# A second level of Strassen-Winograd for two of the seven products in a gate projection

## The chip, the cores and the metric

The kernel runs on one core of a Trainium2 chip. The metric is the device time of one execution in microseconds (us). The engines are TensorE (PE, matrix products), VectorE (DVE), ScalarE (ACT), GpSimd (POOL) and SyncE (SP); DVE, ACT and POOL each work through their instructions in the order of the program, and semaphores make one engine wait for another. DMAs are issued from the queues of SP, ACT and POOL.

## What is computed

With a depth of 1 the reference is one layer, the pooling mixer, between two RMS norms. It has 4096 tokens and a width of 1024, all in float32:

```python
def pool_mixer(h, in_w, group_w, group_b, scale, out_w):
    b, s, _ = h.shape
    u, gate = jnp.split(h @ in_w, 2, axis=-1)
    ug = u.reshape(b, s, POOL_GROUPS, POOL_GROUP_DIM)
    pooled = jnp.stack([trailing_mean(ug[:, :, g], w) for g, w in enumerate(POOL_WINDOWS)],
                       axis=2) - ug
    mixed = jnp.einsum('bsgc,gcd->bsgd', pooled, group_w) + group_b
    y = mixed.reshape(b, s, POOL_WIDTH) * scale * jax.nn.silu(gate)
    return y @ out_w
...
normed = rms_norm(h, norm_w[i])
h = h + pool_mixer(normed, ...)
...
return rms_norm(h, final_norm_w)
```

## The kernel before

**Precision.** Every float32 operand is split in two parts, hi (rounded by an ACT copy, L152) and lo (what is left, a DVE subtraction, L146). A product of operands is three matmuls: hi by hi, hi by lo, lo by hi (`mm3`, L576 to L583). "Splitting" below means such a pair, an ACT copy and a DVE subtraction behind it.

**The seven products.** Each large matrix product is done block by block in the scheme of Strassen and Winograd: the operands are quartered, and seven products P1 to P7 of sums and differences of quarters take the place of eight. P1 is A11 B11 and P7 is S3 T3, where S3 is a difference of quarters of the activations and T3 one of the weights. The activations of one half are two tiles of 128 by 1024.

**Three phases.** First input phase ("a"): the branch that is pooled, 4 blocks of 1024 tokens, with the group map folded into the weights. Second input phase ("b"): the gate, 4 blocks, whose parts of x, normalised in phase a, are read again from memory (`sd`). Output phase ("o"): 8 blocks of 512 tokens. A list of steps (L960 to L962) has 28 products of a, 28 of b and 56 of o; the main loop (L1204) goes through it. In each turn it loads the operands of a step some places ahead, forms sums, splits the operands of the next step, runs the product (`run`, `product_in` at L587) and clears the banks (`evict_in`, L710).

**A product of the input phases** is 48 matmuls of 128 by 512 into four of the eight PSUM banks (`bank_of`, L585: P1, P2, P7 and P4 in banks 0 to 3, the others in banks 4 to 7). Products that follow each other accumulate: P1's result is copied from banks 0 to 3 into 4 to 7 by ACT (L152), P2, P6, P7 and P3 are copied out to SBUF by ACT, P5 and P4 are added to such copies by DVE (L143). In phase b's order, P1, P2, P6, P7, P5, P4, P3, the next block's P1 follows P3.

**Buffers.** The split operands lie in four tiles `op0` to `op3` that are taken in turn (`next_op`, L463), each with hi and lo of one half. All other working tiles come from two sets, 11 `st` tiles and 8 slightly longer `vt` tiles (L112 to L115); a request gets the tile that has been free longest, from the set whose head is older (`take`, L129). A tile's new writer waits for its last reader, a DMA included.

**Statistics.** For blocks 1 to 3 of phase a, the sums of squares come from ACT, the inverse root is finished by POOL (L194 to L212), written to memory (`store_rs`, L421) and read back spread over the partitions (`load_rstd`, L453); both are on POOL's queue. The parts of x are multiplied with it on DVE (`normalize`, L456, its operation at L149) before they are split.

**Weights of phase b** are loaded, formed and split during block 3 of phase a and block 0 of phase b (`load_wb`, `form_wb`, `split_wb`, L262 to L318); T3 is formed and stored earlier (`save_t3`, L274). The output weights are loaded and split in block 3 of phase b (`load_w`, L328).

**The pool stage** (`pool`): the trailing sums as DVE scans (L662), two DVE operations each behind them (L684 and the multiplication at L149), for two groups at once, held back by one or two steps after the product that completes its input (`pool_later`, `pool_due`).

The order of instructions on each engine is made by a scheduler from the program's order; `tc.issue_after` holds an instruction behind another.

Of the kernel before, what the change touches and what calls it, by code (L numbers as in the profile page):

```python
# [10 lines left out]
F32 = mybir.dt.float32  # L11
# [50 lines left out]
def kernel(  # L62
# [48 lines left out]
    ops = [mem.tile([P, 4 * H], F32R, tag=f"op{i}", name=f"op{i}") for i in range(4)]  # L111
# [42 lines left out]
    def split(dst, src):  # L154

        latest_split[1] = copy(dst[:, 0], src).ins
        latest_split[0] = sub(dst[:, 1], src, dst[:, 0].bitcast(F32)).ins
# [10 lines left out]
    wvd = [dram.tile([P, 2, H], F32, name=f"wvd{k}") for k in range(4)]  # L168
    t3d = [dram.tile([P, 2, H], F32, name=f"t3d{h}") for h in range(2)]
# [15 lines left out]
    nc.vector.memset(eps, EPS)  # L185
    scrap = const.tile([P, 1], F32, name="scrap")
# [75 lines left out]
    def load_wb(i):  # L262
        for h in range(2):
            p = parts[i, h] = {}
            if i in (P1, P6):
# [3 lines left out]
            for name, place, used in (("t3", t3d[h], (P6, P7)), ("22", wvd[2 + h], (P5, P3))):  # L269
# [4 lines left out]
    def save_t3():  # L274

        for h in range(2):
# [7 lines left out]
            for u in us:  # L284
                give(u)
# [22 lines left out]
    def split_wb(i):  # L308
        for h in range(2):
            (u,) = parts.pop((i, h)).values()  # L310
            if i == P1:
                split_scaled(w[i][h], u, pair(norm_c, h, 0))
            elif i == P2:
# [147 lines left out]
    turn = [0]  # L461

    def next_op(pattern, **sizes):  # L463
        t = ops[turn[0] % 4]
        turn[0] += 1
        return t.rearrange(pattern, **sizes)
# [3 lines left out]
    def split_halves(us, saved=None, by_pool=False):  # L470
        ts = []
        for h, u in enumerate(us):
            t = next_op("p (s a b) -> p s a b", s=2, a=2)
# [66 lines left out]
    def split_in(q, b, i):  # L540
        s = xs[b]
        key = {P1: "11", P2: "12", P6: "2", P7: "21", P5: "11", P4: "22", P3: "12"}[i]
        later = q == 0 and b == 0 and i in (P1, P2)
# [42 lines left out]

    def product_in(i, t, sets, by_bank, between=None, behind=None):  # L587
        ps = sets[bank_of[i]]
# [3 lines left out]
        for n, (h, ct) in enumerate(halves):  # L592
            if between and n in between:
                between[n]()
            c = slice(ct * P, (ct + 1) * P)
            with tc.issue_after(behind) if behind and n == 1 else nullcontext():
                for kk in range(2):
                    mm3(
                        ps[ct],
                        (w[i][h][:, 0, kk, c], w[i][h][:, 1, kk, c]),  # L600
                        (t[h][:, 0, kk], t[h][:, 1, kk]),
                        i in (P1, P7) and h == 0 and kk == 0,
                        h == 1 and kk == 1,
                    )
        if between and 8 in between:
            between[8]()

# [714 lines left out]
```

## Time and profile before

| | |
|---|---|
| Runs of the kernel before | median 916.3 us, 915.63 to 917.7 (3 runs) |
| The profiled execution | 917.32 us, its span 915.6 us |
| Granted TensorE clock | 0.998 |
| Matmuls 128x512 of the input phases (`bank<-op,w`) | 2688 |
| Read from and written to memory | 115.45 MB and 60.83 MB |
| Second input phase in the trace | about 329 to 620 us |

A row of a group has the line, the engine, the operation, what is written and read (buffer numbers left out), the tile shapes and the count; then its busy time in us, the mean ns of one, and the idle time of its engine just before, with what ended it. Matmuls are pipelined, so the mean of one is longer than their spacing. A row of a timeline has the start and the duration in us. A row of DMA issues has the queue, the count, the KB of one and the median us from the issue to the landing. A row of windows has the window and, for each engine, busy us and instructions.

### The profile page before, as it was taken

What the parts mean: (1) busy time and instruction counts of PE and PEld (TensorE: products, weight loads), DVE (VectorE), ACT (ScalarE), POOL (GpSimd) and SP (SyncE); (2) the same over time, 40 slices, a digit from 0 to 9 for tenths busy, and PEclk for the clock granted to TensorE, in tenths of its full rate; (3) what the DMA queues carried; (4) which work ended last, traced back from release to release, by engine and by line L of the source; (5) the groups of instructions that cost most, each with busy time, mean ns of one, the idle gap of its engine ahead of it and who ended that gap; (6) DMA issues with size and microseconds to landing.
All of it is one profiled execution on the core that took longest, in us unless ns stands there. A gap on an engine that the chain in (4) does not pass through costs nothing.

```text
span 915.6 us, 11210 instructions
## 1 busy us (share of the span) xinstructions
PE 904.4 (99%) x4212; PEld 789.0 (86%) x4212; DVE 703.5 (77%) x769; ACT 457.5 (50%) x741; POOL 52.6 (6%) x130
## 2 busy tenths in 40 slices
PE   9999999999999999999999999999999999999996
PEld 7788888888888888888888888888888888888886
DVE  3898994894699997586696589589978677676675
ACT  7869447447345565246345546654423424324333
POOL 0023201001100000000000000000101101001010
PEclk9999999999999999999999999999999999999999
DMA  9986865666756635016614725745746536356122
GB/s 340 401 320 195 316 236 166 214 230 197 264 198 241 250 146 200 24 47 238 244 47 160 257 87 194 246 161 184 252 165 227 163 135 230 128 194 216 37 92 93
DMA packets 66518, 177.02 MB, mean 193 GB/s; under 512 B 6048, under 2 KB 23840, under 8 KB 66464
## 3 DMA queue, kind: packets, MB, share of 16 engines
q1 hardware_dynamic: 59888, 154.78, 47.9%
q10 hardware_dynamic: 4176, 13.65, 3.8%
q0 software_dynamic: 2400, 7.88, 2.5%
q8 instruction: 33, 0.54, 0.2%
q14 instruction: 21, 0.17, 0.1%
HBM read 115.45 MB, written 60.83 MB: 193 GB/s over the span
## 4 chain that ended last, share of the span: by engine, by line
PE 88%; DMA 5%; DVE 3%; ACT 2%; issue 1%; SPq 0%; DVEq 0%; ACTq 0%
PE bank L581 88%; DMA early<-in_wut 2%; DMA st<-in_x 1%; DMA st<-wvd 1%; DMA st<-in_xt 1%; DVE op L146 1%; DMA t3d<-st 1%; PE bank L374 0%; DVE st L146 0%; DVE st L149 0%; ACT early L408 0%; ACT op L152 0%; DVE st L143 0%; DVE vt L143 0%; DVE vt L146 0%
## 5 line engine op out<-in xcount | busy, mean ns | idle before, releaser
L581 PE MATMUL bank<-op,w 128*128 128x512 f32 x2688 | 581.8, 379 | 2.3 <-DVE op L146 1.5
L581 PEld LDWEIGHTS bank<-op,w 128*128 128x128 f32 x2688 | 507.6, 189 | 75.7 <-DVE op L146 2.3
L581 PE MATMUL bank<-w,op 128*128 128x512 f32 (+1 forms) x1356 | 290.3, 377 | 0.0
L581 PEld LDWEIGHTS bank<-w,op 128*128 128x128 f32 x1356 | 254.6, 189 | 35.8
L146 DVE TENSOR_TENSOR op<-st,op 128x1024 fp32r<-128x1024 f32 x127 | 154.6, 1221 | 75.6 <-ACT op L152 75.5
L152 ACT ACTIVATE op<-st 128x1024 fp32r<-128x1024 f32 x127 | 133.1, 1052 | 143.8 <-PE bank L581 128.5
L152 ACT ACTIVATE vt<-bank 128x512 f32<-128x512 f32 x100 | 56.8, 593 | 49.3 <-PE bank L581 42.4
L152 ACT ACTIVATE op<-vt 128x1024 fp32r<-128x1024 f32 x39 | 40.9, 1055 | 78.8 <-PE bank L581 65.7
L924 DVE TENSOR_TENSOR st<-bank,st 128x512 f32<-128x512 f32 x60 | 41.1, 687 | 29.8 <-PE bank L581 29.4
L146 DVE TENSOR_TENSOR st<-st,st 128x1024 f32<-128x1024 f32 x35 | 42.5, 1221 | 19.3 <-DMA st<-sd 8.6
L146 DVE TENSOR_TENSOR op<-vt,op 128x1024 fp32r<-128x1024 f32 x39 | 47.5, 1222 | 9.5 <-ACT op L152 9.5
L194 POOL TENSOR_SCALAR oms<-oss 128x2 f32<-128x2 f32 x14 | 9.2, 658 | 600.0 <-ACT st L813 593.9
L152 ACT ACTIVATE bank<-bank 128x512 f32<-128x512 f32 x48 | 27.8, 580 | 30.7 <-PE bank L581 27.1
L146 DVE TENSOR_TENSOR w<-st,w 128x1024 fp32r<-128x1024 f32 x21 | 25.5, 1221 | 12.4 <-ACT w L152 12.3
L662 DVE TENSOR_TENSOR_SCAN vt<-vt,bf 128x512 f32<-128x512 f32 x28 | 34.5, 1269 | 0.2 <-ACT vt L152 0.2
L143 DVE TENSOR_TENSOR vt<-bank,vt 128x512 f32<-128x512 f32 (+1 forms) x51 | 33.2, 678 | 1.6 <-PE bank L581 1.6
L924 DVE TENSOR_TENSOR vt<-bank,vt 128x512 f32<-128x512 f32 (+1 forms) x37 | 24.8, 673 | 12.0 <-PE bank L581 11.7
L152 ACT ACTIVATE w<-st 128x1024 fp32r<-128x1024 f32 x21 | 21.9, 1053 | 17.9 <-PE bank L581 14.9
L149 DVE TENSOR_TENSOR st<-st,vt 128x1024 f32<-128x1024 f32 x23 | 27.2, 1219 | 3.1 <-DMA st<-in_xt 3.1
L684 DVE SCALAR_TENSOR_TENSOR vt<-vt,vt 128x1024 f32<-128x1024 f32 x24 | 29.1, 1214 | 0.0
L152 ACT ACTIVATE st<-bank 128x512 f32<-128x512 f32 x30 | 17.5, 595 | 22.7 <-PE bank L581 10.8
L817 DVE SCALAR_TENSOR_TENSOR st<-st,ors,st 128x1024 f32<-128x1024 f32 x17 | 21.4, 1281 | 6.1 <-POOL ors L212 6.1
(130 smaller groups left out, 556.0 us busy)
## 6 DMA issues: line engine op xcount, KB each, us to landing
st<-in_x SPq DMA_DIRECT2D x36, 512.0 KB, 5.0
st<-in_xt SPq DMA_DIRECT2D x29, 512.0 KB, 6.6
st<-sd SPq DMA_DIRECT2D x29, 512.0 KB, 5.0
sd<-st ACTq DMA_DIRECT2D x23, 512.0 KB, 3.7
vt<-in_x SPq DMA_DIRECT2D x21, 512.0 KB, 5.1
st<-yd SPq DMA_DIRECT2D x19, 512.0 KB, 4.3
yd<-vt SPq DMA_DIRECT2D x18, 512.0 KB, 2.8
out<-st SPq DMA_DIRECT2D x17, 512.0 KB, 3.6
```

The lines of the kernel that those rows point to most:

```text
L143: nc.vector.tensor_tensor(out=dst, in0=a, in1=b, op=ALU.add)
L146: return nc.vector.tensor_tensor(out=dst, in0=a, in1=b, op=ALU.subtract)
L149: nc.vector.tensor_tensor(out=dst, in0=a, in1=b, op=ALU.mult)
L152: return nc.scalar.activation(dst, src, func)
L194: nc.gpsimd.tensor_scalar(out=ms, in0=ss, scalar1=1.0 / D, scalar2=EPS, op0=ALU.mult, op1=ALU.add)
L581: latest[0] = nc.tensor.matmul(ps, a, b, start=start and n == 0, stop=stop and n == 2, skip_group_check=True).ins
L662: nc.vector.tensor_tensor_scan(s[:, j, at:end], v[:, j, at:end], v[:, j, at - win : end - win], sums_of[j] if sums_of else 0.0, ALU.add, A ...
L684: nc.vector.scalar_tensor_tensor(out=s[:, :, at : at + H], in0=s[:, :, at : at + H], scalar=1.0 / win, in1=v[:, :, HIST:], op0=ALU.mult, o ...
L817: nc.vector.scalar_tensor_tensor(out=us[j], in0=us[j], scalar=rs[:, j : j + 1], in1=fw[0], op0=ALU.mult, op1=ALU.mult,)
L924: partial["added"] = nc.vector.tensor_tensor(out=dst, in0=src, in1=dst, op=ALU.add).ins
```

## The change

P1 and P7 of every block of phase b are each computed by seven inner products, by the same scheme applied once more (`mm_inner`): 84 matmuls of 128 by 256 take the place of 48 of 128 by 512, in the order P1, P7, P6, P2, P5, P4, P3. v11, v12, v21 and v22 are the quarters of the result; v11 and v21 lie in the two halves of banks 0 and 1, v12 and v22 in those of banks 2 and 3. The inner products accumulate in place: ACT clears two quarters first, copies v11 to v12 after the inner P1 and v22 to SBUF (m7) after the inner P7; DVE adds v12 and m7 into v21 and later into v22. The last three of the eight units of the preceding product (six matmuls of 128 by 512 each) are placed between the inner products (`fill`).

The inner operands are four new sums and seven splits of 512 columns, in place of two splits of 1024. The operand tiles become eight of half the size. The inner weights are made once: for P1 after step P6 of block 1 of phase a, for P7 after step P5 of block 2 (`store_wi`: four sums, seven splits and seven stores of 512 KB on POOL's queue each). Before each inner product, seven tiles of 512 KB are read again on POOL's queue (`load_wi`), for P1 after step P5 of the preceding block, for P7 after step P2. The old preparation of the weights of P1 and P7 is left out, T3 stays in SBUF until its `store_wi`, and the output weights of P1 and P7 are loaded at steps P7 and P5 of the last block.

```diff
-    ops = [mem.tile([P, 4 * H], F32R, tag=f"op{i}", name=f"op{i}") for i in range(4)]
+    ops = Slots([mem.tile([P, 2 * H], F32R, tag=f"op{i}", name=f"op{i}") for i in range(8)])
...
+    def split_inner(ms):
+        us, sums_in, ts = inner["us"], inner["sums"], inner["ops"]
+        q = {(h, th): quarter(us, h, th) for h in range(2) for th in range(2)}
+        for m in ms:
+            if m == P7:
+                tiles = [take("p (m a b) -> p m a b", m=2, a=2) for _ in range(2)]
...
+                sub(sums_in[P7], q[0, 0], q[0, 1])
...
+            ts[m] = ops.take(lambda t: t.rearrange("p (s a b) -> p s a b", s=2, a=2))
+            split((by_side(ts[m][:, 0]), by_side(ts[m][:, 1])), src)
...
+    def mm_inner(m, banks_of, j, th):
+        t, wm = inner["ops"].pop(m), wi[M_ORDER.index(m)]
+        for c in range(2):
+            ps = banks_of[2 * j + c][:, th * 256 : (th + 1) * 256].rearrange(
+                "p (a s) -> p a s", s=2
+            )
+            cols_of = slice(c * P, (c + 1) * P)
+            for kk in range(2):
+                for n, (sw, sr) in enumerate(((0, 0), (0, 1), (1, 0))):
+                    latest[0] = nc.tensor.matmul(
+                        ps, wm[:, sw, kk, cols_of],
+                        t[:, sr, kk].rearrange("p (s a) -> p a s", s=2),
...
+    def inner_product(i, sets, fill):
+
+        ps = sets[bank_of[i]]
+        v11, v12, v21, v22 = part(ps, 0, 0), part(ps, 1, 0), part(ps, 0, 1), part(ps, 1, 1)
+        mm_inner(P1, ps, 0, 0)
+        split_inner([P3])
+        for c in range(2):
+            copy(v12[c], v11[c])
+        mm_inner(P7, ps, 1, 1)
+        m7 = inner["tiles"][0][:, 0]
+        for c in range(2):
+            copy(m7[:, c], v22[c])
+        fill.pop(0)()
+        mm_inner(P6, ps, 1, 0)
+        for c in range(2):
+            add(v21[c], v12[c], m7[:, c])
+        mm_inner(P2, ps, 0, 0)
+        fill.pop(0)()
+        mm_inner(P5, ps, 1, 0)
+        for c in range(2):
+            add(v22[c], v12[c], m7[:, c])
+        give(inner["tiles"][0])
+        mm_inner(P4, ps, 0, 1)
+        fill.pop(0)()
+        mm_inner(P3, ps, 1, 0)
...
+    def load_wi(i):
+        for m in range(7):
+            nc.gpsimd.dma_start(out=wi[m], in_=wid[i][m])
+
+    def store_wi(i, us):
+
+        t = [take("p (m a b) -> p m a b", m=2, a=2) for _ in range(2)]
...
+        with tc.issue_after(latest_split[0]):
+            sub(t1, b12, b11)
+            sub(t2_, b22, t1)
+            sub(t3, b22, b12)
+            sub(t4, b21, t2_)
+        src = {P1: b11, P2: b21, P3: b22, P4: t4, P5: t1, P6: t2_, P7: t3}
+        behind = latest_split[0]
+        for n, m in enumerate(M_ORDER):
+            u = take("p (s a b) -> p s a b", s=2, a=2)
+            r = u.bitcast(F32R)
+            with tc.issue_after(behind):
+                copy(r[:, 0], src[m])
+                sub(r[:, 1], src[m], u[:, 0])
+            nc.gpsimd.dma_start(out=wid[i][n], in_=r)
+            give(u)
...
+        elif is_inner(n):
+            evict_in(b, 1, i, sets)
+        elif is_inner(n + 1):
+            t = split_up.pop(n)
+            clear_inner(steps[n + 1][2], sets)
+            for ct in range(4):
+                unit(i, t, sets, 0, ct)
+            give_ops(t[0])
+            split_inner(M_ORDER[4:6])
+            unit(i, t, sets, 1, 0)
+            inner_product(
+                steps[n + 1][2], sets, [lambda ct=ct: unit(i, t, sets, 1, ct) for ct in (1, 2, 3)]
+            )
...
+        if kind == "a" and b == 1 and i == P7:
+            raw = []
+            for h in range(2):
+                raw.append(load_rows(in_w, 2 * h, D + H))
+                scale_rows(raw[h], pair(norm_c, h, 0))
+        elif kind == "a" and b == 1 and i == P6 or kind == "a" and b == 2 and i == P5:
+            store_wi(P1 if b == 1 else P7, raw)
+            for u in raw:
+                give(u)
         if kind == "a" and b == 2 and i == P6:
-            save_t3()
+            raw = save_t3()
...
+        if kind == "b" and i == P2:
+            load_wi(P7)
+        if kind == "b" and i == P5 and b + 1 < NB:
+            load_wi(P1)
```

More of the change, by code (lines that the diff above doesn't have):

```diff
@@ L168 @@
     wvd = [dram.tile([P, 2, H], F32, name=f"wvd{k}") for k in range(4)]
+    wid = {
+        i: [dram.tile([P, 2, 2, H // 2], F32R, name=f"wid{i}_{m}") for m in range(7)]
+        for i in (P1, P7)
+    }
     t3d = [dram.tile([P, 2, H], F32, name=f"t3d{h}") for h in range(2)]
@@ L274, in save_t3 @@
     def save_t3():
+        t3 = []
         for h in range(2):
@@ L460, with next_op, give_ops @@
     xs = [{} for _ in range(NB)]
[L461 to L466, printed above, removed]
+    def next_op(a):
+        return tuple(
+            ops.take(lambda t: t.rearrange("p (a b) -> p a b", a=a)) for _ in range(2)
+        )
+    def give_ops(ts):
+        for u in ts:
+            ops.give(u)
     first_saves = []
@@ L542, in split_in @@
         key = {P1: "11", P2: "12", P6: "2", P7: "21", P5: "11", P4: "22", P3: "12"}[i]
+        if q and i in INNER:
+            inner.update(us=s[key], sums={}, ops={})
+            split_inner(M_ORDER[:4])
+            return None
         later = q == 0 and b == 0 and i in (P1, P2)
```

121 lines of the change are left out of this document (94 added, 27 removed).

## The prediction

> **What bounds the kernel now.** I read the page's first two parts, then the waits of TensorE, then the groups by line.
>
> ```profile
> span 915.6 us, 11210 instructions
> PE 904.4 (99%) x4212; PEld 789.0 (86%) x4212; DVE 703.5 (77%) x769; ACT 457.5 (50%) x741; POOL 52.6 (6%) x130
> PE   9999999999999999999999999999999999999996
> PEclk9999999999999999999999999999999999999999
> ...
> L581 PE MATMUL bank<-op,w 128*128 128x512 f32 x2688 | 581.8, 379 | 2.3 <-DVE op L146 1.5
> ...
> PE bank L581 <- DVE op L146: 1.5, 2, 1.0
> ```
>
> TensorE is busy 99% of the span at the full granted clock; its largest wait, for a split, is 1.5 us in all. So only fewer or shorter matmuls can shorten the kernel, and whatever makes PE wait lengthens it at once. A 512-wide matmul costs 581.8/2688 = 0.2164 us, a product of 48 of them 10.39 us (the 379 ns is one matmul's own, pipelined, duration). DVE at 77% is the engine with the least room behind it. In the phase that is changed:
>
> ```profile
> 278.00:351.00 73.00, 72.97 (x338) 63.59 (x337) 70.75 (x76) 41.13 (x58) 0.00 (x0) 1.00 0.61 219
> 351.00:423.00 72.00, 72.00 (x335) 63.04 (x335) 50.76 (x54) 35.92 (x60) 0.00 (x0) 1.00 0.24 89
> 423.00:496.00 73.00, 73.00 (x340) 63.93 (x339) 52.12 (x50) 33.98 (x65) 0.00 (x0) 1.00 0.43 160
> 496.00:568.00 72.00, 72.00 (x336) 63.04 (x335) 52.24 (x49) 36.56 (x69) 0.00 (x0) 1.00 0.53 190
> ```
>
> These are windows of about one block each (busy us of PE, PEld, DVE, ACT, POOL; then clock, DMA share, GB/s). The second input phase runs from about 329 to 620. DVE has 20 us of slack in a block, and almost none in the window before it.
>
> **1. Matmuls.** Eight products (P1 and P7 of four blocks) go from 48 matmuls of 512 columns to 84 of 256. The kernel has two kinds of 256-wide matmul:
>
> ```profile
> L581 PE MATMUL bank<-w,op 128*128 128x256 f32 x24 | 2.8, 275 | 0.0
> L374 PE MATMUL bank<-w,w 128*128 128x256 f32 x48 | 6.2, 288 | 0.0
> ```
>
> The last of a run stays its own duration, the others their spacing: (2.8-0.275)/23 = 0.110 us, the same woven operand form as here, and (6.2-0.288)/47 = 0.126 us. I take 0.110: an inner product costs 84 x 0.110 = 9.24 us and saves 1.15, eight save 9.2; at 0.126 it costs 10.58 and eight lose 1.5. Every matmul here has its own weight load (4212 of each on the page), in these two groups as in the inner product, so the spacings hold the load too. I put in -8.9, rounded for the shorter runs of six.
>
> A rule of the Trainium skill speaks against the change: TensorE: Matmul & The Clock Gate, section Back-to-back issue gap, gives 131 ns for 512 columns and 81 for 128; a straight line between gives an estimate of 98 ns for 256, by which 84 x 0.098 = 8.2 us would stand against 48 x 0.131 = 6.3, so eight products would lose 15. The row of 2688 matmuls shows 216 ns where the page has 131, so it does not hold for this kernel and the sum goes by the rows.
>
> **2. The stores of the inner weights.** They are made once: four sums and seven (ACT copy, DVE subtraction, POOL store of 512 KB) for P1 in block 1 of the first phase, and the same for P7 in block 2. In the planned order of the changed kernel all seven pairs of P1 use one and the same vt buffer. Copy n+1 therefore waits until store n has landed, and the load of block 2's rstd, also into that buffer and on POOL's queue, is behind the seventh. Block 2's P1 needs that rstd. Where these stand in the trace of before:
>
> ```profile
> 148.33 0.57 POOL L421 DMA_DIRECT2D rd<-rs  x1 [0.41 <-POOL rs L212]
> 153.16 0.57 POOL L453 DMA_DIRECT2D vt<-rd  x1 [4.26 <-DMA rd<-rs]
> ...
> 145.30 0.30 ACT L193 ACTIVATE tmp<-ss,eps 128x4 f32<-128x4 f32 x1
> ...
> 184.40 0.58 ACT L152 ACTIVATE bank<-bank 128x512 f32<-128x512 f32 x1 [0.55 <-PE bank L581]
> ...
> sd<-st POOLq DMA_DIRECT2D x6, 512.0 KB, 4.6
> wvd<-early POOLq DMA_DIRECT2D x4, 512.0 KB, 5.5
> vt<-rd POOLq DMA_DIRECT2D x6, 256.0 KB, 5.7
> sd<-st ACTq DMA_DIRECT2D x23, 512.0 KB, 3.7
> sd<-vt ACTq DMA_DIRECT2D x1, 512.0 KB, 2.6
> ...
> L146 DVE TENSOR_TENSOR op<-st,op 128x1024 fp32r<-128x1024 f32 x127 | 154.6, 1221 | 75.6 <-ACT op L152 75.5
> L152 ACT ACTIVATE op<-st 128x1024 fp32r<-128x1024 f32 x127 | 133.1, 1052 | 143.8 <-PE bank L581 128.5
> ```
>
> The first copy stands in ACT's order right behind the square root of 145.30; copy and subtraction end about 147.9, and the first store issues behind the rstd store, at about 148.9. One trip is the landing (4.6, POOL's median for 512 KB), a copy and a subtraction of 512 columns (half of 1.05 and of 1.22 and a little: 1.25) and about 0.35 of hand-overs: 6.2 us. The seventh store lands at 148.9 + 4.6 + 6 x 6.2 = 190.7, the rstd load 5.7 later at 196.4; with its hand-over, then normalisation (1.2), hi copy (1.05) and lo subtraction (1.2) PE gets block 2's P1 at about 200. Before, P1 began a bank (12 matmuls, 2.6 us) ahead of the bank copy at 184.40, at 181.7. Stall: **18.3 us**. Nothing covers it, since no other product is ready. Every microsecond of landing moves it by 7: 14.8 at 4.1 (0.5 under the median), 24.6 at 5.5 (the row of wvd), 4.3 at 2.6 (the fastest 512 KB store, another queue). I take 4.6, the nearest row in queue and size; the DMA engines are 47 to 90% busy there:
>
> ```profile
> 145.00:155.00 10.00, 10.00 (x48) 8.77 (x47) 2.27 (x4) 7.66 (x13) 2.86 (x6) 1.00 0.47 140
> 155.00:165.00 10.00, 10.00 (x49) 8.74 (x48) 7.20 (x10) 4.11 (x11) 2.13 (x7) 1.00 0.80 265
> 175.00:185.00 10.00, 10.00 (x48) 8.77 (x47) 7.63 (x9) 5.37 (x11) 0.00 (x0) 1.00 0.90 289
> ```
>
> The Trainium skill (DMA: Bandwidth & Descriptors, section Anatomy of one DMA) puts such a transfer at 2.0 us and its bytes over 436 GB/s, 3.2 us here as an estimate; by it the stall would be 8.5 and my time 9.8 lower. The rows for 512 KB on this queue are all longer.
>
> The stores of P7 alternate between two st buffers, and only one stands ahead of block 3's rstd load. Block 3's P1 waited 0.96 us of the 1.5 above and may lose that wait; two x loads behind the last stores may cost up to 2. I take -0.5, between -1 and +2.
>
> **3. Hand-overs in an inner product.** Its operands need 7 pairs of 512 columns and four sums in place of two pairs of 1024: DVE 11 x 0.65 against 2 x 1.2, and four adds of 256 columns in PSUM, some 7 us more for each product, 14 a block: DVE goes from 52 to 66 of 72 us. It has room, but the order matters. The inner P2 writes the banks of v21 and must wait for DVE's adds into v21; DVE works in order, and in its planned order a whole pool stage and the remaining splits stand ahead of them. Worked out for block 2's P1, with DVE's rows of before:
>
> ```profile
> 462.43 1.31 DVE L143 TENSOR_TENSOR vt<-bank,vt 128x512 f32<-128x512 f32 x2
> 464.19 1.23 DVE L146 TENSOR_TENSOR op<-st,op 128x1024 fp32r<-128x1024 f32 x1 [0.45 <-ACT op L152]
> 465.45 1.22 DVE L143 TENSOR_TENSOR st<-st,st 128x1024 f32<-128x1024 f32 x1
> 466.59 3.63 DVE L662 TENSOR_TENSOR_SCAN vt<-vt,bf 128x512 f32<-128x512 f32 x3
> 470.14 1.20 DVE L684 SCALAR_TENSOR_TENSOR vt<-vt,vt 128x1024 f32<-128x1024 f32 x1
> 471.25 1.28 DVE L662 TENSOR_TENSOR_SCAN vt<-vt,bf 128x512 f32<-128x512 f32 x1
> 472.45 1.20 DVE L149 TENSOR_TENSOR vt<-vt,vt 128x1024 f32<-128x1024 f32 x1
> 473.56 1.22 DVE L684 SCALAR_TENSOR_TENSOR vt<-vt,vt 128x1024 f32<-128x1024 f32 x1
> 474.70 1.22 DVE L146 TENSOR_TENSOR op<-st,op 128x1024 fp32r<-128x1024 f32 x1
> 475.83 1.22 DVE L149 TENSOR_TENSOR vt<-vt,vt 128x1024 f32<-128x1024 f32 x1
> ...
> L152 ACT ACTIVATE bank<-bank 128x512 f32<-128x512 f32 x48 | 27.8, 580 | 30.7 <-PE bank L581 27.1
> L143 DVE TENSOR_TENSOR vt<-bank,vt 128x512 f32<-128x512 f32 (+1 forms) x51 | 33.2, 678 | 1.6 <-PE bank L581 1.6
> ```
>
> P4 ends with the last add from PSUM, at 463.6, and P3 starts. PE needs the add after P3's first 30 matmuls (6.5), two inner products of 12 (2.65), a fill of 6 (1.3) and the inner P6 (1.3): 475.4. DVE, from 463.7, has four lo subtractions (0.6 each), the eight pool instructions (466.59 to 476.97 less the split at 474.70: 9.25) and a 1024-wide sum (1.15): the first v21 add starts at 476.5, the second behind another 1.15. With 0.42 for an add of 256 columns (from 0.678 for 512) the second ends near 478.6, while the six matmuls between take 0.66: PE loses 2.5 us. The same count gives 2 to 3 for blocks 0 and 3, 3 to 3.7 for block 1, and for P7, whose pool stage stands earlier, 3, 1, 0.3 and 2. All eight: **16 us**. From below 0: with free engines two ACT copies and the adds (about 2.5 us) fit under the fill and the inner P6 (2.6). From above 30: the largest, 3.7, at each.
>
> **4. The rest** costs nothing on PE. The inner weights are read again by POOL's queue, 8 x 3.67 MB, 29 MB in 290 us, 100 GB/s on top of 89 to 190, with DMA shares of 0.24 to 0.53 in the windows above; each tile is freed some 26 us before its next use, against landings of 5. Without that cover a late tile would stop PE for one landing. P1's and P7's old weight preparation (four pairs of 1024 columns) leaves DVE, where the window to 351 is full; that relief is in the tallies for block 0. The output weights of P1 and P7 are loaded two to four products later, still two products ahead.
>
> **Sum.** 917.3 (the profiled execution's own time; span 915.6 and 1.7 around it) - 8.9 + 18.3 + 16 - 0.5 = 942.2. The median of the runs shown, 916.3, is 1.0 lower: **941 us**.
>
> **Rivals.**
> - Only the setup stalls: the fills cover every hand-over. For it: DVE's slack of 20 us a block; against: its fixed order at the rows above. 916.3 - 8.9 + 18.3 - 0.5 = 925.
> - DVE becomes the bound of the phase: one late product makes the next one's splits late, and each inner product loses 5 us more than tallied for half of them. For it: 66 of 72 us busy; against: plain products between let DVE catch up. 941 + 4 x 5 = 961.
> - The other side: the trip through the one buffer is short. The stall goes to 0 when a store lands within 2.0 us; at 2.6 it is 4.3. If it lands so fast and hand-overs stay at 4 or less, 916.3 - 8.9 + 0 + 4 - 0.5 = 911, up to 915 with 2.6. It speaks for it that these are plain stores of 4 KB rows, and against it that no row of POOL's is under 4.1.
> - The change does not save on PE: 256 columns cost 0.126. 941 + 10.4 = 951.
>
> **How the numbers follow.** Forecast 0.60 (its own bounds: 14.8 and 0 added to 24.6 and 30, with the small terms 922 to 962); setup alone 0.12; DVE bound 0.10; no saving on PE 0.08; short trip 0.10. The range 920 to 964 takes in all but the short trip and the outer ends. A difference under 0.2% (1.8 us) can't be told from none for this kernel: faster 0.09, same 0.03 (small stalls that just meet the saving), slower 0.88.
>
> **What would show it.** In the changed profile: inner matmuls as a group with 84 x 8 = 672 entries at about 0.110 us each; a gap of PE near 181 to 200, ended by a DVE split whose chain goes over an rstd load and POOL stores of six-microsecond spacing; gaps of 2 to 4 us inside P1's inner products ended by DVE's PSUM add (L143); no wait of PE for weight rereads. The prediction is wrong if the gap at 181 is under 7 us, if the stores do not follow one another singly, or if PE waits in the second phase for 30 us or for none.

## The result and the profile after

| | before | changed |
|---|---|---|
| median of 4 runs | 916.23 us | 985.8 us (983.58 to 989.59) |
| ratio to before | | 1.0761, 95% interval 1.0722 to 1.08 |
| the profiled execution, its span | 917.32, 915.6 us | 987.3, 985.5 us |

The change makes the kernel 69.5 us slower. The prediction had 941 us and at most 964: the sign was right, the time was not. First the lines of the page of the changed kernel that answer to those of before (engines, busy tenths and granted clock in 40 slices, then groups of matmuls and TensorE's waits):

```profile
span 985.5 us, 12298 instructions
PE 923.9 (94%) x4500; PEld 808.7 (82%) x4500; DVE 758.3 (77%) x890; ACT 495.8 (50%) x857; POOL 92.6 (9%) x200
PE   9999998679998999999898898989999999999997
...
PEclk9999999979998999999899998999999999999999
...
L595 PE MATMUL bank<-op,w 128*128 128x512 f32 x2304 | 520.9, 386 | 29.0 <-ACT op L152 16.5
L678 PE MATMUL bank<-op,wi 128*128 128x256 f32 x672 | 95.6, 296 | 24.7 <-ACT bank L152 17.5
...
PE bank L678 <- ACT bank L152: 17.5, 8, 4.5
PE bank L595 <- ACT op L152: 16.5, 1, 16.5
PE bank L595 <- ACT st L152: 4.7, 1, 4.7
PE bank L678 <- DVE bank L143: 4.6, 3, 2.5
```

Three things are to be seen. TensorE is idle for 985.5 - 923.9 = 61.6 us where it was 11.2. Its busy time rose too, by 19.5 us, though there is less to multiply. And the granted clock, 9 in every slice before, has gaps of its own where PE has them: the mean fell from 0.998 to 0.968.

**Where PE waits.** TensorE's timeline has some 17 gaps; these are the large ones of the first phase and one of the second. A row is the stretch that follows the gap, with the gap and what ended it in brackets:

```profile
158.81 28.95 PE L595 MATMUL bank<-op,w 128*128 128x512 f32 x126 [4.74 <-ACT st L152]
204.28 77.14 PE L595 MATMUL bank<-op,w 128*128 128x512 f32 x343 [16.52 <-ACT op L152]
283.83 12.10 PE L595 MATMUL bank<-op,w 128*128 128x512 f32 x47 [2.42 <-DVE op L146]
...
302.45 57.69 PE L595 MATMUL bank<-op,w 128*128 128x512 f32 x252 [2.77 <-ACT bank L152]
...
369.44 0.83 PE L678 MATMUL bank<-op,wi 128*128 128x256 f32 x6
...
477.04 1.65 PE L678 MATMUL bank<-op,wi 128*128 128x256 f32 x6 [4.54 <-ACT bank L152]
...
569.35 2.84 PE L678 MATMUL bank<-op,wi 128*128 128x256 f32 x24
```

The last row is an undisturbed stretch: (2.84 - 0.275)/23 = 0.1115 us for an inner matmul, as was forecast. Six of them take 0.83 us at 369.44, where nothing waits, and 1.65 us at 477.04, right behind a gap: twice as long.

**What the gaps cost beside themselves.** Windows around the longest one (columns as before; behind POOL the granted clock, DMA share, GB/s):

```profile
188.00:196.00 8.00, 0.00 (x0) 0.00 (x0) 4.39 (x6) 2.42 (x5) 0.53 (x1) 0.79 0.76 257
196.00:204.00 8.00, 0.00 (x0) 0.00 (x0) 2.09 (x2) 0.83 (x1) 1.11 (x2) 0.50 0.73 268
204.00:208.00 4.00, 3.73 (x9) 3.00 (x10) 4.00 (x5) 1.49 (x3) 0.00 (x0) 0.50 0.68 266
208.00:212.00 4.00, 4.00 (x17) 3.34 (x16) 4.00 (x4) 2.66 (x7) 0.00 (x0) 0.80 0.66 262
215.00:230.00 15.00, 15.00 (x71) 13.15 (x70) 15.00 (x16) 4.27 (x6) 0.00 (x0) 1.00 0.52 194
```

In the idle window the clock falls to 0.50, and it stays there for the first five microseconds of work: 9 matmuls start in the 3.73 us from 204.28, one every 0.43 us, where it is 0.216 at full clock. Then it is 1.00 again. This is what the Trainium skill states (TensorE: Matmul & The Clock Gate, section What's actually happening): after an idle window of about 3.4 us the clock is halved, until a busy window has passed. For this gap of 16.5 us the trace agrees. The clock record, from 130 to 700 us, has 0.5 only around the gaps, in pieces of 3.4 us and multiples of it:

```
from (us)     158.4 192.6 284.7 301.8 445.2 475.9 523.7 564.6 605.6 643.1
length (us)     3.4  17.1   3.4   6.8   3.4   6.8   3.4   3.4   6.8   3.4
```

For shorter gaps the runs differ from that statement. Here every gap from 2.15 us on has such a piece and no gap up to 1.62 us has one, so a gap need not last 3.4 us. And in `e11_gpsimd` a gap of 3.15 us, ending at 288 us, has none: a gap of two to three microseconds may or may not cost clock.

For an account I took every distance between the starts of two matmuls from 130 us to the end of the second phase, less 0.2158 us for 512 columns or 0.1117 for 256. Of a distance over 0.8 us the excess counts as a gap, that of shorter ones as slow matmuls:

```
us                     first phase      second phase
                       gaps   slow      gaps   slow
before                  1.1    0.4       0.0    0.0
changed kernel         28.2    9.6      26.2   15.9
```

That is 78.4 us more, against 69.9 us of span, which leaves 8.5 us for what the shorter products save. By the two spacings they save 8 x (48 x 0.2158 - 84 x 0.1117) = 7.8 us, so the account closes to within 0.7 us. Of the 25.5 us of slow matmuls some 22 stand in the pieces at half clock.

**The chain of the stores** is as forecast. POOL's timeline, then ACT's and DVE's where they are held:

```profile
149.32 0.57 POOL L428 DMA_DIRECT2D rd<-rs  x1 [0.41 <-POOL rs L219]
149.95 0.56 POOL L753 DMA_DIRECT2D wid<-vt  x1
159.40 0.53 POOL L753 DMA_DIRECT2D wid<-vt  x1 [8.90 <-DVE vt L146]
165.60 0.53 POOL L753 DMA_DIRECT2D wid<-vt  x1 [5.66 <-DVE vt L146]
...
190.25 0.53 POOL L753 DMA_DIRECT2D wid<-vt  x1 [4.87 <-DVE vt L146]
196.97 1.11 POOL L460 DMA_DIRECT2D vt<-rd  x2 [6.18 <-DMA wid<-vt]
```

```profile
157.65 0.63 ACT L152 ACTIVATE vt<-vt 128x512 fp32r<-128x512 f32 x1 [8.12 <-DMA wid<-vt]
158.18 0.58 ACT L152 ACTIVATE st<-bank 128x512 f32<-128x512 f32 x1
...
475.51 0.72 ACT L239 ACTIVATE st<-st,colt 128x512 f32<-128x512 f32 x1 [1.79 <-DMA st<-in_out_w]
476.14 0.58 ACT L152 ACTIVATE vt<-bank 128x512 f32<-128x512 f32 x1
476.62 0.38 ACT L152 ACTIVATE bank<-bank 128x256 f32<-128x256 f32 x1
```

```profile
201.91 2.36 DVE L149 TENSOR_TENSOR st<-st,vt 128x1024 f32<-128x1024 f32 x2 [9.48 <-DMA vt<-rd]
```

Six trips from 149.95 to 190.25 are 6.7 us each on the mean, between 4.8 and 9.7; the stores themselves land 2.9 to 7.9 us after their issue. rstd lands at 201.9 and P1 follows. But ACT's second copy, waiting 8.12 us for the first store, holds up the eviction behind it (158.18), and PE stops 4.74 us at P5: a stall that was not in the sum. In the second phase ACT's copy of v11 (476.62) stands behind a scaling of the output weights that waits 1.79 us for its load, and PE waits 4.54 us for the copy.

### The profile page after: what moved, and what is told of

It reads as the page before. It is cut to its first block, busy times and chain, and to the rows that moved or that the text cites. A ratio compares the mean times of both kernels' runs of the same rounds, so it can differ in the third digit from the quotient of the medians.

```text
span 985.5 us, 12298 instructions
## 1 busy us (share of the span) xinstructions
PE 923.9 (94%) x4500; PEld 808.7 (82%) x4500; DVE 758.3 (77%) x890; ACT 495.8 (50%) x857; POOL 92.6 (9%) x200
## 4 chain that ended last, share of the span: by engine, by line
PE 48%; DVE 24%; DMA 11%; issue 8%; ACT 8%; POOL 1%; DVEq 0%; ACTq 0%; SPq 0%; POOLq 0%
PE bank L595 42%; DVE op L146 5%; PE bank L678 4%; DVE st L146 2%; DVE vt L143 2%; DVE st L149 2%; DVE vt L812 2%; ACT op L152 2%; DMA wid<-vt 2%; DVE vt L834 2%; DVE vt L146 2%; DMA st<-in_out_w 1%; ACT vt L152 1%; DMA st<-wvd 1%; DMA st<-in_in_w 1%
## 5 line engine op out<-in xcount | busy, mean ns | idle before, releaser
L595 PE MATMUL bank<-op,w 128*128 128x512 f32 x2304 | 520.9, 386 | 29.0 <-ACT op L152 16.5
L595 PEld LDWEIGHTS bank<-op,w 128*128 128x128 f32 x2304 | 440.2, 193 | 93.8 <-ACT op L152 16.9
L152 ACT ACTIVATE op<-st 128x1024 fp32r<-128x1024 f32 (+1 forms) x144 | 133.0, 933 | 160.4 <-PE bank L595 89.3
L146 DVE TENSOR_TENSOR op<-st,op 128x1024 fp32r<-128x1024 f32 (+1 forms) x144 | 152.9, 1071 | 39.8 <-ACT op L152 35.8
L678 PE MATMUL bank<-op,wi 128*128 128x256 f32 x672 | 95.6, 296 | 24.7 <-ACT bank L152 17.5
L678 PEld LDWEIGHTS bank<-op,wi 128*128 128x128 f32 x672 | 91.4, 208 | 33.1 <-ACT bank L152 19.6
L152 ACT ACTIVATE op<-vt 128x1024 fp32r<-128x1024 f32 (+1 forms) x62 | 58.3, 944 | 90.2 <-PE bank L595 64.3
L146 DVE TENSOR_TENSOR op<-vt,op 128x1024 fp32r<-128x1024 f32 (+1 forms) x62 | 66.8, 1083 | 12.4 <-ACT op L152 12.3
L152 ACT ACTIVATE vt<-bank 128x512 f32<-128x512 f32 (+1 forms) x100 | 55.7, 578 | 37.4 <-PE bank L595 32.3
L146 DVE TENSOR_TENSOR st<-st,st 128x1024 f32<-128x1024 f32 (+2 forms) x46 | 46.6, 1023 | 19.2 <-ACT st L239 6.9
L152 ACT ACTIVATE st<-bank 128x512 f32<-128x512 f32 (+1 forms) x46 | 24.7, 545 | 22.6 <-PE bank L595 11.8
L143 DVE TENSOR_TENSOR vt<-bank,vt 128x512 f32<-128x512 f32 (+1 forms) x49 | 32.0, 677 | 0.8 <-PE bank L595 0.6
```

What stands on the lines that cost most here:

```text
L143: nc.vector.tensor_tensor(out=dst, in0=a, in1=b, op=ALU.add)
L146: return nc.vector.tensor_tensor(out=dst, in0=a, in1=b, op=ALU.subtract)
L152: return nc.scalar.activation(dst, src, func)
L595: latest[0] = nc.tensor.matmul(ps, a, b, start=start and n == 0, stop=stop and n == 2, skip_group_check=True).ins
L678: latest[0] = nc.tensor.matmul(ps, wm[:, sw, kk, cols_of], t[:, sr, kk].rearrange("p (s a) -> p a s", s=2), start=False, stop=kk == 1 and ...
```

## The experiments

Each run is compared with the kernel before on the same chip (915.6 to 916.7 us). The account by the same rule for all of them, with the median:

```
us                          median   first phase    second phase
                                     gaps   slow    gaps   slow
changed kernel              985.8    28.2    9.6    26.2   15.9
e1_once                     971.0    14.7    3.0    32.6   14.2
e2_busy                     991.4    13.2    6.8    33.3   12.6
e3_nohand                   977.3    24.9    8.6    22.3   14.5
e4_plain                    955.6    25.4   10.2     2.5    1.7
e5_order                    985.6    27.2    5.9    26.6   14.5
e6_wo                       984.2    26.9    9.1    23.9   16.5
e7_spread                   975.0     8.0    3.1    36.9   16.6
e8_all                      958.1    12.0    5.3    20.9   11.7
e9_nopool                   961.9    26.3    8.8    11.1    5.1
e10_poolafter               965.1    12.3    3.7    25.2   12.4
e11_gpsimd                  972.9    10.5    2.7    37.9   16.1
e12_bothless                938.1     9.9    2.2    13.2    7.1
```

The first theory was: setup stalls, hand-overs inside the inner products, and a slow clock behind both.

**e4_plain: the setup alone**

```diff
     def is_inner(n):
-        kind, _, i = step(n)
-        return kind == "b" and i in INNER
+        return False
...
             load_wi(P1)
+            w[P1] = w[P7] = [whole[P1][0], whole[P1][1]]
```

> P1 and P7 of the second phase are plain products of 48 matmuls again, with the reread tiles in place of their weights (wrong values); the stores and the rereads of the inner weights stay. Theory: only the setup stalls are left, 28 us idle and 10 us slow, on a kernel of 916: 952 to 956 us. Rival (rereading 29 MB collides with other transfers and costs by itself): above 965 us. Rival (setup stalls are small without the inner products): under 940 us.

Measured 955.6 us, ratio 1.0426 (1.0396 to 1.0456). The forecast of 952 to 956 holds: without any inner product the kernel is 39 us slower, 34 of them gaps and slow matmuls of the first phase, where the inner weights are prepared. The rereads, which this kernel keeps, cost nothing that shows: the second phase has one gap, of 2.5 us, and no wait of PE in this run ends with a reread. What is left for the inner products is 985.8 - 955.6 = 30 us (31.6 between the profiled spans): 40 us of gaps and slow matmuls less some 8 us saved.

**e2_busy: the clock**

```diff
+            if kind == "a" and b == 2 and i == P1:
+                for _ in range(76):
+                    latest[0] = nc.tensor.matmul(
+                        banks[0], warm[:, 0:P], warm, start=True, stop=True,
+                        skip_group_check=True,
+                    ).ins
             product_in(i, split_up.pop(n), sets, i == P1, between, behind)
```

> 76 matmuls of 128x512 in bf16, written into a free bank ahead of block 2's P1, fill the gap of 16.5 us near 188 us; the result is not touched. Theory (an idle TensorE loses its clock): the gap is as long as before, but the matmuls behind it run at 0.216 us from the first on; in the changed kernel they lost 2.9 us there, so about 983 us, and the granted clock of 200 to 215 us rises from 0.68 to 1.00. Rival (the matmuls behind a gap are slow because of memory traffic or late operands): 986 us, the pace behind the gap stays.

Windows of this run, and TensorE's timeline around the place:

```profile
200.00:215.00 15.00, 15.00 (x71) 10.37 (x69) 12.69 (x12) 4.74 (x8) 0.00 (x0) 1.00 0.58 224
206.00:210.00 4.00, 4.00 (x20) 3.31 (x19) 4.00 (x4) 1.74 (x2) 0.00 (x0) 1.00 0.50 201
```

```profile
190.04 16.80 PE L1173 MATMUL bank<-const-bfloat16-1.0 128*128 128x512 bf16 x76
206.49 21.36 PE L595 MATMUL bank<-op,w 128*128 128x512 f32 x96
```

The clock stays at 1.00, and behind the place some 20 matmuls run in 4 us, where the changed kernel has 9. The DMA share from 200 to 215 us is no lower here (0.58) than in the changed kernel (0.52 for the same window of its own trace), so memory traffic does not explain the slow ones: the clock does. The mechanism is shown, but the forecast of 983 us is missed: 991.4 against 985.8. The second phase, which the edit leaves alone, had 33 us of gaps in place of 26. Every edit can change the scheduler's order there, so differences of a few microseconds between these runs prove nothing.

**e1_once: no copy waits for a store**

```diff
+        u = take("p (s a b) -> p s a b", s=2, a=2)
+        r = u.bitcast(F32R)
+        with tc.issue_after(behind):
+            copy(r[:, 0], src[P1])
+            sub(r[:, 1], src[P1], u[:, 0])
         for n, m in enumerate(M_ORDER):
-            u = take("p (s a b) -> p s a b", s=2, a=2)
...
             nc.gpsimd.dma_start(out=wid[i][n], in_=r)
```

> Each of the two preparations of inner weights computes one pair and stores that one tile seven times, so that no copy waits for a store; the inner weights are wrong, everything else is as in the changed kernel. Theory (setup stalls, each with a slow clock behind it): the gaps near 154, 187 and 281 to 300 us go, 28 us of idle time and 10 us of slow matmuls, so about 948 us. Rival (the slow matmuls are not a matter of the gaps): only the idle time goes, about 958 us. Rival (the rstd load is late for another reason): above 975 us.

Measured 971.0 us: missed, between the forecasts of 958 and 975. Half of the first phase's gaps stay. POOL's timeline of this run:

```profile
151.64 3.20 POOL L753 DMA_DIRECT2D wid<-vt  x6
156.12 0.54 POOL L753 DMA_DIRECT2D wid<-vt  x1 [1.29 <-issue]
...
175.77 0.60 POOL L460 DMA_DIRECT2D vt<-rd  x1 [14.64 <-DMA wid<-vt]
```

Without the trips the last store, issued at 156.1, still needs until about 175 to land, 3.67 MB in some 24 us, and the rstd load still waits for them, since it goes into the same buffer. So the single trips are not the whole harm: the shared buffer and the place in the queue remain. This run does not weigh one against the other.

**e7_spread: the same weights, stored elsewhere**

```diff
-        if kind == "a" and b == 1 and i == P7:
+        if kind == "a" and b == 1 and i == P5:
...
-            store_wi(P1 if b == 1 else P7, raw)
-            for u in raw:
-                give(u)
+            to_store.extend(wi_pairs(P1, raw))
+        elif kind == "a" and b == 2 and i == P5:
+            to_store.extend(wi_pairs(P7, raw))
+        if kind == "a" and (b, i) not in ((1, P5), (2, P5)):
+            for _ in range(min(2, len(to_store))):
+                to_store.pop(0)()
...
+        sums = {
+            P5: ((b11, b12, b11), (b12, b22, b12)),
+            P6: ((b22, b22, b11),),
+            P4: ((b21, b21, b22),),
+        }
...
+            u = take("p (s a b) -> p s a b", s=2, a=2)
+            r = u.bitcast(F32R)
+            with tc.issue_after(evicted[0]), tc.issue_after(latest_split[0]):
+                for args in sums.get(m, ()):
+                    sub(*args)
+                copy(r[:, 0], src[m])
+                sub(r[:, 1], src[m], u[:, 0])
+            nc.gpsimd.dma_start(out=wid[i][M_ORDER.index(m)], in_=r)
```

> The changed kernel with the same inner weights stored in another way: sums in place, two pairs a step through different tiles, P1's from step P4 of block 1 on (behind the loads of rstd), P7's from step P4 of block 2 on; the result is the reference's. Theory (the setup costs what the run with plain products shows, 39 us, through buffers and queue order, not through the work): 946 to 952 us. Rival (the setup's own work on ACT, DVE and the DMA engines costs too): 955 to 965 us. Rival (the first-phase gaps are not the stores'): above 975 us.

The first phase did what was expected, from 37.8 to 11.1 us of gaps and slow matmuls. The time is 975.0, not 950: the second phase, whose own instructions the edit leaves alone, rose from 42 to 53.5. Of the 312 DVE instructions there in the changed kernel, 290 stand in the same sequence in both kernels; the others were placed anew by the scheduler. Whether the new order or the earlier arrival made the second phase worse is not shown. The number fits the rival of over 975 us, its reason does not: the first phase's gaps were the stores'.

**e3_nohand, e5_order, e6_wo: is it the hand-overs?**

```diff
-        for c in range(2):
-            copy(v12[c], v11[c])
...
-            copy(m7[:, c], v22[c])
...
-            add(v21[c], v12[c], m7[:, c])
...
-            add(v22[c], v12[c], m7[:, c])
```

> The copies of v11 and v22 and the additions into v21 and v22 are left out of every inner product; all matmuls, splits, stores and rereads stay. Theory (the hand-overs between PE, ACT and DVE inside an inner product cost 25.6 us of idle time and some 15 us of slow matmuls): about 945 us. Rival (the splits are late, since DVE is full, and the hand-overs only wait behind them): above 965 us. Rival (the 256-wide matmuls themselves are slow): 970 us, their spacing stays above 0.13 us on the mean.

Measured 977.3 us, missed by 32: the gaps of the second phase fall only from 26.2 to 22.3, and PE's waits there are now mostly those of ordinary products. This fits the rival of late splits; the other rival, slow 256-wide matmuls, is out by the spacing of 0.1115 us above. One of the waits, in the timelines of ACT and PE of this run:

```profile
490.59 0.72 ACT L239 ACTIVATE st<-st,colt 128x512 f32<-128x512 f32 x1 [4.14 <-DMA st<-in_out_w]
...
493.73 0.59 ACT L152 ACTIVATE st<-bank 128x512 f32<-128x512 f32 x1
...
494.38 2.93 PE L595 MATMUL bank<-op,w 128*128 128x512 f32 x6 [4.76 <-ACT st L152]
```

```diff
-    M_ORDER = (P1, P7, P6, P2, P5, P4, P3)
+    M_ORDER = (P7, P1, P2, P6, P5, P4, P3)
...
+        mm_inner(P1, ps, 0, 0)
+        for c in range(2):
+            copy(v12[c], v11[c])
+        fill.pop(0)()
+        fill.pop(0)()
+        mm_inner(P2, ps, 0, 0)
+        mm_inner(P6, ps, 1, 0)
```

> The changed kernel with the inner products in the order P7, P1, P2, P6, P5, P4, P3 and four units of the preceding product as fill, two of them between the inner P1 and what waits for the copy of v11: the cover of ACT's copies goes from nothing to 2.6 us or more, the cover of DVE's additions to 1.3 us each; the result is the reference's. Theory (PE waits directly for ACT's copies, which are 2 to 5 us late): the 25.6 us of idle time inside the inner products fall to about 12 and the slow matmuls behind them from 15 to 8 us: about 965 us. Rival (the splits themselves are late, as the run without hand-overs suggests, and the waits only move): 980 to 988 us.

985.6 us: missed, the rival holds. The inner matmuls' waits for ACT's bank copies shrink (17.5 to 6.2 us), and waits for splits (3.0 to 11.8 us at ordinary products) and for DVE's additions (4.6 to 6.8 us) take their place.

```diff
-                scale_rows(us[kh, n], pair(scale_c, h, kh))
+                with tc.issue_after(evicted[0]):
+                    scale_rows(us[kh, n], pair(scale_c, h, kh))
```

> The changed kernel with the scaling of the output weights (ACT, waits for a late load) held behind the eviction of P7, so that it no longer stands ahead of the copies and splits of P7's inner product in blocks 1 and 2; the result is the reference's. Theory (a long wait of another ACT instruction, hidden before the change, is handed to PE): the gaps of 4.5 us at 472 and of 1.0 and 2.2 us at 557 to 564 go, with 4 us of slow matmuls: 974 to 978 us. Rival (ACT is late there for another reason): 983 to 988 us.

984.2 us: missed, the rival's range, and no different from the changed kernel's 983.6 to 989.6. The gap of 4.54 us near 472 became one of 2.8. Taking hand-overs away, covering them and moving another wait: each time most of the wait was handed on. The theory of the hand-overs fell; a new one was that DVE has too much to do around the inner products.

**e9_nopool: DVE's load**

```diff
             s = take_v()
             at = HIST
+            if q:
...
+                continue
             if win == 2:
```

> The changed kernel without DVE's work of the pool stage in the second phase (scans, differences and products of eight stages; the stores and ACT's small copies stay, the output is not the reference's). Theory (what stands on DVE ahead of the splits and additions of an inner product sets its waits): idle time inside the second phase falls from 25.6 to under 10 us, the slow matmuls behind it from 15 to 5: 958 to 965 us. Rival (ACT's order alone sets them): 980 to 986 us.

961.9 us, as expected: gaps and slow matmuls of the second phase fall from 42 to 16 us, with the order of the inner products as it was. DVE is not full on the mean (65.17 of 78 us in a window of the changed kernel), but pool stages of some 9 us stand ahead of what PE needs within a few. Rows of the changed kernel: the window, ACT's waits for the scans, then P1 of block 2, in the timelines of ACT, DVE and PE:

```profile
366.00:444.00 78.00, 74.54 (x425) 65.82 (x423) 65.17 (x86) 43.13 (x74) 8.45 (x16) 1.00 0.60 201
...
ACT junk L793 <- DVE vt L812: 16.1, 14, 3.7
...
521.11 0.31 ACT L793 ACTIVATE junk<-tails,colt 128x16 f32<-128x16 f32 x1 [0.51 <-DVE vt L812]
523.20 0.37 ACT L152 ACTIVATE bank<-bank 128x256 f32<-128x256 f32 x1
...
518.62 3.63 DVE L812 TENSOR_TENSOR_SCAN vt<-vt,bf 128x512 f32<-128x512 f32 x3
530.81 0.43 DVE L143 TENSOR_TENSOR bank<-bank,st 128x256 f32<-128x256 f32 x1
...
531.29 0.94 PE L678 MATMUL bank<-op,wi 128*128 128x256 f32 x6 [1.57 <-DVE bank L143]
```

DVE's addition at 530.81 is behind the pool stage that begins at 518.62, and ACT's copy of v11 at 523.20 is behind small ACT sums (L793) that wait for the same scans. Such waits were in the kernel before too, 15.2 us of them, and cost PE nothing there. In `e9_nopool` they are gone, and the pool stage's tiles can come free earlier as well. So the run shows that DVE's pool work is the cause of 26 of these 42 us; it does not tell DVE's own order, ACT's waits for it and the buffers apart.

**e8_all, e10_poolafter, e11_gpsimd, e12_bothless: can it be had?** `e8_all` joins e5, e6 and e7, with the inner copies and additions at high priority:

```diff
-        for c in range(2):
-            copy(v12[c], v11[c])
+        with tc.high_priority():
+            for c in range(2):
+                copy(v12[c], v11[c])
```

> The three edits together (inner order with four fills, output weight scaling held back, stores spread), and ACT's copies and DVE's additions of the inner products at high priority in the planned order; the result is the reference's. If the three act on separate gaps: 985.8 - 38 - 20 - 9 = 919 us, and with the priority some 5 less. If the clock alone explains the sum (each gap avoided gives its slow matmuls back): 910 to 920 us. If DVE's and ACT's load sets the second phase: above 930 us.

958.1 us, the best of the kernels that compute the reference, but far above the 919 of separate gaps and the 910 to 920 of the clock alone: the third case, a second phase set by the load of DVE and ACT, fits. With ACT's copies covered, the wait that the prediction described stands there, 2.4 to 3.7 us where it had 2 to 3.7 (TensorE's timeline, P1 of blocks 1 to 3):

```profile
431.14 2.93 PE L679 MATMUL bank<-op,wi 128*128 128x256 f32 x12 [2.39 <-DVE bank L143]
...
509.99 2.93 PE L679 MATMUL bank<-op,wi 128*128 128x256 f32 x12 [3.58 <-DVE bank L143]
...
587.48 2.35 PE L679 MATMUL bank<-op,wi 128*128 128x256 f32 x12 [3.71 <-DVE bank L143]
```

`e10_poolafter` takes the pool stage out of its way:

```diff
-        pool_due(n)
+        if not is_inner(n + 1):
+            pool_due(n)
...
         mm_inner(P3, ps, 1, 0)
+        with tc.issue_after(added[0]):
+            pool_due(n)
...
-            u = take("p (s a b) -> p s a b", s=2, a=2)
+            u = take("p (s a b) -> p s a b", st if st.free else None, s=2, a=2)
```

> The kernel of the three edits together (958.1 us) with two more: the pool stage due at P3 is held behind the last addition of P1's inner product, and the stores of inner weights are staged in st tiles, not in the vt tiles that the evictions need; the result is the reference's. Theory (DVE's order, and buffers in the first phase): the waits for the additions at P1 (9.7 us in three blocks) go with 5 us of slow matmuls, and most of the 10 us near 205 us too: 930 to 942 us. Rival (the wait moves to the next product's splits, behind the same pool stage): 950 to 960 us.

965.1 us, ratio 1.0519 (1.0387 to 1.0651): the rival, or worse. The waits for the additions are gone and stand at splits and evictions behind the same pool stage (25.2 us of gaps in place of 20.9). In the first phase, with st tiles as staging, one wait of 11.5 us near 212 took the place of two.

`e11_gpsimd` has the four sums of each inner product as GpSimd operations in place of DVE's:

```diff
+    def on_pool(dst, a, b, op):
+        nc.gpsimd.tensor_tensor(out=dst, in0=a, in1=b, op=op)
...
-                sub(sums_in[P7], q[0, 0], q[0, 1])
+                on_pool(sums_in[P7], q[0, 0], q[0, 1], ALU.subtract)
```

> The kernel of the three edits together (958.1 us) with the four operand sums of each inner product on GpSimd, which is idle 90% of the time, in place of DVE; the result is the reference's. Theory (DVE's work around the inner products sets the waits): 2.4 us less for DVE at each of eight products, of which half reaches PE: 945 to 952 us. Rival (GpSimd's sums are late themselves, behind its rereads in its queue, or slow DVE down): 955 to 975 us.

972.9 us: the rival. A row by form of GpSimd's operations in this run:

```profile
L152 POOL TENSOR_TENSOR st<-st,st 128x512 f32<-128x512 f32 x12 | 17.2, 1434 | 17.0 <-DVE op L146 16.5
```

These twelve sums take 1.4 us on the mean, all 32 between 1.3 and 4.5 us, and on DVE such a sum takes 0.69 (L146 and L143 in the changed kernel). PE's gaps in the second phase rise to 37.9 us.

`e12_bothless` is e8_all with the edit of e9_nopool:

> The kernel of the three edits together (958.1 us) without DVE's work of the pool stage in the second phase; the output is not the reference's. Theory (DVE's work, and not the order alone, keeps the second phase from its gain): idle time and slow matmuls there go from 33 us to under 8, and with the first phase's rest (13 us idle, 6 slow) the kernel takes 930 to 938 us. Rival (the shorter inner products leave PE waiting for ACT in any order): above 945 us.

938.1 us (ratio 1.0244, 1.0184 to 1.0304), at the upper end of what was expected, but partly by luck: the second phase has 20 us of gaps and slow matmuls where under 8 were expected, and the first phase, which this edit leaves alone, has 12 where 19 were. Of the 20, 17 stand before 380 us, in block 0, where DVE and ACT also prepare weights; behind that there are two gaps, of 2.0 and 0.8 us. So without DVE's pool stages the later blocks do run nearly without waits. No version here comes near 916 us, and even with no stall at all the change could give only some 8 us.

## Why the prediction was wrong, step by step

**Matmuls: right.** 0.110 us was forecast for an inner matmul and 0.1115 measured; -8.9 us forecast, -7.8 by the two spacings. The estimate from two figures of the Trainium skill (TensorE: Matmul & The Clock Gate, section Back-to-back issue gap), rightly set aside in the prediction, would have made it a loss of 15 us.

**The setup: mechanism right, size half.** The chain, its trip (6.2 us forecast, 6.7 measured) and the stall at block 2's P1 (18.3 forecast, 16.5) came as described. That the mean trip came so close has some luck in it: a median landing of 4.6 stood for landings of 2.9 to 7.9 us, and single 512 KB stores on POOL's queue had landed in 3.1 us before the change too (issued at 50.6 us), so the rival of a short trip was set aside too firmly. Missing were the stall of 4.7 us at P5, where ACT's waiting copy stands ahead of an eviction, and 6 us around block 3's P1, where the sum had -0.5: ACT waits for P7's stores, and x loads wait behind them for tiles. I had looked at what waits for the stores' data, not at all that stands behind a waiting instruction in ACT's order. Gaps in all: 27.1 us added, against 17.8. The run with plain products shows the whole, slow matmuls included, at up to 39.

**The hand-overs: wait and size off.** The sum had 16 us of waits for DVE's additions; 26.2 were measured, most of them (17.5 us on the page) for ACT's bank copies, above all that of v11, which has no fill to cover it: the inner P7 follows the inner P1 at once and writes the banks that the copy writes. And the picture behind it, single hand-overs with a cover, was wrong: leaving all of them out gave 4 us less of gaps, and covering them none. What sets the phase is DVE's work with its pool stages, which holds splits, evictions and ACT alike (26 us of gaps and slow matmuls went with them). The rival of DVE as the bound came nearest to this, at 961 us and a chance of 0.10, and its time too was 25 us short.

**The step that failed altogether: the price of a gap.** The sum took a microsecond of waiting as a microsecond lost and had no term for what follows a gap. It is more: 53.3 us of added gaps came with 25.1 us of added slow matmuls, most of them at half the clock. With the corrections the sum gives the measured time to within a microsecond: 942.2 + 1.1 (matmuls) + 9.3 (setup) + 10.2 (second phase) + 25.1 (clock) = 987.9, against 987.3 for the profiled execution. Without the clock's term it is 962.8, still inside the range of 920 to 964, so it is this missing term that takes the time out of the range.

Little in the profile of before could show it: its clock is 9 in every slice, and its longest wait of TensorE is 1.0 us. The one sign stands at its start, where eight matmuls of 512 columns run ahead of the work (the clock record begins behind them, at 4.7 us):

```profile
L1026 PE MATMUL bank<-const-bfloat16-1.0 128*128 128x512 bf16 x8 | 3.6, 625 | 0.8 <-PEq L1307 0.8
```

They are (3.6 - 0.625)/7 = 0.43 us apart, the spacing that the changed kernel has behind its longest gap. The rule of the Trainium skill named above (TensorE: Matmul & The Clock Gate, section What's actually happening) could have given a term for the stall of 18.3 us, and the prediction did not use it; for the hand-overs, forecast at 0.3 to 3.7 us, it would have given little, and there the runs show more than it states.

**The rest: right.** PE never waits for a reread, and the run with plain products shows them without cost.

## What to carry to other kernels

A change that shortens the work of an engine that is busy 99% of the time can win only what it shortens, here some 8 us, and pays for every wait it makes, in these runs about 1.4 to 1.5 times on the whole. So count first how many new points there are at which that engine must have an answer from another one within a few microseconds, and look at what stands ahead of the answer in that engine's order, waits for DMAs included; their length in the old profile says nothing as long as a whole product of 10 us covered them. Moving single instructions about hardly helped (`e3_nohand`, `e5_order`, `e6_wo`); three such edits together with priority brought the second phase from 42 to 33 us of gaps and slow matmuls, and leaving out the answering engine's other work brought it to 16. Handing a part of that work to a slower engine did not help.

## What the runs showed of the hardware that was not expected

Behind TensorE's idle gaps of 2.15 us and more the changed kernel's clock record has 0.5 in pieces of 3.4 us, and the matmuls behind such a gap lost 1.6 to 3.8 us in all; gaps up to 1.62 us had no such piece. In other runs some gaps of two to three microseconds had none either, one of 3.15 us among them. Filling a gap of 16.5 us with matmuls that nobody needs kept the clock at 1.00. 512 KB stores on POOL's queue landed 2.9 to 7.9 us after their issue, with a mean trip of 6.7 us through one buffer, and seven issued together took some 24 us to land. GpSimd needed 1.3 to 4.5 us for a sum of two 128x512 tiles where DVE needed 0.69.
